# One-core block kernel: time-step work of the first stage ahead of the last S5 tile, more S5 buffers, residual reloads by GpSimd

## The chip, the cores and the metric
The kernel runs on one core of a Trainium2 chip. The metric is the time of one execution in device microseconds, the median of several runs. The engines that matter here are TensorE (PE in the rows; its weight loads are PEld), VectorE (DVE), ScalarE (ACT), GpSimd (POOL) and SyncE (SP), which only issues transfers. Each engine works through its own list of instructions in order.

## The reference
A sequence of 512 tokens with 16 meta tokens ahead of it (528 in all), 1024 wide, goes through a first block with two mixers side by side, then through a two-layer latent and context transformer. The change lies in the first block. Cut to what matters:
```python
xbc = silu(conv(...)); dt = softplus(dt_raw + dt_bias)       # SSD mixer
a_cs = cumsum(dt * -exp(a_log))                              # per chunk
y = y_diag + y_off + x * d;  y = rmsnorm(y * silu(z))
bu = u @ bb;  s = associative_scan(a, bu)                    # S5 mixer, complex, 64 groups
y5 = gelu(s_re @ c_re - s_im @ c_im + u * d_skip)
v = y5 @ w_glu + b_glu;  y5 = rmsnorm(v[:D] * sigmoid(v[D:]))
h = x + out_proj(concat(y, y5))                              # then an MLP
```

## The kernel before, in words
All matrix products are in float32, each as three matmuls of a high and a low part (`mm3`, lines 247 to 249). A weight tile arrives as `raw` (line 233, a transfer of SyncE, two buffers), ScalarE casts its high part `whi` (L239), VectorE subtracts for the low part `wlo` (L241).

The first stage follows `ORDER` (L207), a string that `build` works through letter by letter: x is one of twelve tiles of the convolution input with its silu (`xbc_proj`, L562 to L567), z one of four steps of the gate z (four silus, L592), P and S prepare and scan one of eight S5 tiles, d is the time-step projection with its softplus (`dt_proj`), e its cumulative sums (`dt_scan`, tiles acs and acsx), r the result of one S5 tile (`s5_result`). Engine order is made from this program order by a scheduler that weighs priorities and free buffers, and is then fixed.

`s5_scan` of a tile: angles (DVE f, ACT sine pieces L784 to L786), S on TensorE (L873) in two halves, each copied by ScalarE (L875) and permuted on TensorE (Sp, L877), rotated on VectorE (L878 to L880), the scan (L885), a permutation Zp (L888), rotation back (L889 to L891), y on TensorE (L894, L896), the copy ye (L899) and its write to a scratch tensor yD in DRAM (L900). `s5_result` reads it back in another layout as yt (L906), applies the gelu (L908), and makes high and low parts y50h, y50l and so on (L912, L913). These feed the gated linear unit, whose matmuls carry the names glug and glua and run over all eight y tiles. The tiles are numbered 0 to 7; tile 7 is the last.

The pools: `S2` is the number of 576-element buffers that S5 tiles, angles and yt share, `B4` that of the 1152-element ones. `hT` are the eight residual tiles. In the first stage they lend their space to S5 inputs and to z and the SSD state, and `ssd_out` loads the residual into them again (L698), for the addition behind the output projection (L958, L959).

ScalarE has a load instruction (ACT_TABLE_LOAD) ahead of a function whose table is not the one in use. Silu and sine follow each other here without one; exp and gelu each have their own.

Of the kernel before, what the change touches and what calls it, by code (L numbers as in the profile page):

```python
# [20 lines left out]
META = 16  # L21
# [169 lines left out]
class Builder:  # L191
# [12 lines left out]
    UB = (1, 0)  # L204
    MB = 0
    GL = (1, 2, 1, 2, 2)
    ORDER = "xPPxSPxSxPSxPxSPSzPSxxPSxzxxSrrzrxdrzrrrre"  # L207
    NF = (1, 0)
    SIDE = (1, 2, 2)
    FILL = (2, 2, 2, 2)  # L210
# [474 lines left out]
    def ssd_out(self):  # L685

        T = self.nc.tensor
        out = []
        for f in range(8):
            ps = self.mps(f"yT{f}")  # L690
            for i in range(1, 5):
                T.transpose(ps[:, (i - 1) * P:i * P],
                            self.ys[i, f // 4][:, (f % 4) * P:(f % 4 + 1) * P], self.C("ident"))
            out.append(self.split(f"mA{f}", ps, self.vec("g_ssd", f), tag="f"))
            self.tap(f"yssd{f}", out[-1][0].bitcast(F32))
        self.mixA = out
        for k in range(8):
            self.nc.sync.dma_start(self.hT[k][:, META:], self.I["xT"][k][:, META:])  # L698


    def s5_tables(self):
# [948 lines left out]
    def build(self, upto="all"):  # L1650
        tc = self.tc
        from contextlib import ExitStack
        with ExitStack() as st:
            self.kp = st.enter_context(tc.tile_pool(name="kp", bufs=1))
            self.wp = st.enter_context(tc.tile_pool(name="wp", bufs=3))
            self.dp = st.enter_context(tc.tile_pool(name="dp", bufs=1, space=DRAM))
            self.mod = {}
            self.tags = {"r": (TOK, 16), "f": (TOK, 16)}
            self.S2, self.B4 = 16, 8
            self.SM = 80  # L1660
            with tc.tile_pool(name="gp", bufs=4, space=PSUM) as self.gp, \
                    tc.tile_pool(name="sp", bufs=12) as self.sp, \
                    tc.tile_pool(name="mp", bufs=4, space=PSUM) as self.mp, \
                    tc.tile_pool(name="ap", bufs=1) as self.ap, \
                    tc.tile_pool(name="bp", bufs=1) as self.bp:
                self.setup()
                self.ys, self.xbcT, self.y5 = {}, {}, []
                self.in_proj()
                order = [8, 9, 10, 11, 0, 1, 2, 3, 4, 5, 6, 7]
                mats, z = {}, self.z_proj()  # L1670
                np_, ns = 0, 0
                for step in self.ORDER:
                    if step == "P":
                        mats[np_] = self.s5_prepare(np_)
                        np_ += 1
                    elif step == "S":
                        self.s5_scan(ns, mats.pop(ns))
                        ns += 1
                    elif step == "d":
                        self.dt_proj()  # L1680
                    elif step == "e":
                        self.dt_scan()
                    elif step == "x":
                        self.xbc_proj(order.pop(0))
                    elif step == "z":
                        next(z)
                    elif step == "r":
                        self.s5_result(len(self.y5))
                self.prev = [self.hT[2 * g + 1][:, :512] for g in range(2)]
                self.tags.update(b4=(1152, self.B4), s2=(576, self.S2))  # L1690
                side = self.ada(0, "s2", "b4", "s2", range(self.ADA1))
                g = self.glu()
                for i in range(5):
                    self.ssd_chunk(i)
                    for _ in range(self.GL[i]):
                        next(g)
                for _ in g:
                    pass
                self.out_proj(1, self.mixB, side)
                self.ssd_out()  # L1700
                self.out_proj(0, self.mixA, side)
                for _ in side:
                    pass
            for k in range(8):
                self.tap(f"hmix{k}", self.hT[k])
            self.SM = 16
            self.cxp = st.enter_context(tc.tile_pool(name="cxp", bufs=1))
            self.setup2()
            self.tags = {"h": (SEQ, 16), "gt": (SEQ, 14), "qk": (SEQ, 8), "vb": (SEQ, 4),
                         "kx": (SEQ + CTX, 2), "p": (SEQ, 4), "cv": (SEQ, 4), "yf": (SEQ, 4), "t": (SEQ, 6),  # L1710
                         "u": (SEQ + 30, 3), "b": (CTX, 3)}
            with tc.tile_pool(name="gp2", bufs=3, space=PSUM) as self.gp, \
                    tc.tile_pool(name="sp2", bufs=16) as self.sp, \
                    tc.tile_pool(name="mp2", bufs=5, space=PSUM) as self.mp, \
                    tc.tile_pool(name="ap2", bufs=1) as self.ap:
                side = self.ctx_stream()
                credit, step = 0.0, None
                for _ in self.mlp():
                    credit += 1.0
                    while credit > 0 and step != "last":  # L1720
                        step = next(side)
                        credit -= self.PACE.get(step, 0.0)
                for k in range(8):
                    self.tap(f"hmlp{k}", self.hT[k])
                self.second_block(side)


# [11 lines left out]
```

## Time and profile before
| | |
|---|---|
| runs | 2740.95, 2732.67, 2740.70 us; median 2740.7 |
| profiled execution | 2738.33 us, span 2736.6 us |
| busy in the span | TensorE 98%, VectorE 75%, ScalarE 43% |
| first stage | up to some 317 us of the span |

The times are those of whole executions; the span is what the trace covers of one of them. A busy share of 98% is a mean over the span: the gaps of TensorE have to be read from the stretch in which they lie.

### The profile page before, as it was taken

The numbers are of one execution on the slowest core, as the hardware profiler recorded it, in microseconds if no ns is written. First come the engines' busy times: TensorE is split into PE (matmuls) and PEld (weight loads), VectorE is DVE, ScalarE is ACT, GpSimd is POOL, SyncE is SP. The second block draws the span as 40 slices with busy tenths as digits, with TensorE's granted clock in tenths as the row PEclk, the third lists the DMA queues.
The fourth block names the chain that finished last, engine by engine and source line by source line (L and its number), as shares of the span: only waits on it lengthen the run. The fifth ranks groups of instructions, "written<-read, shape, count | busy, mean of one in ns | idle before, by whom it ended". The sixth has DMA issues, their size and how long they took to land.

```text
span 2736.6 us, 39800 instructions
## 1 busy us (share of the span) xinstructions
PE 2675.2 (98%) x15107; PEld 2269.9 (83%) x15107; DVE 2041.1 (75%) x3986; ACT 1165.5 (43%) x1961; POOL 6.0 (0%) x52
## 2 busy tenths in 40 slices
PE   8999899999999999999999999999999999999998
PEld 8898678788887898777788888888887777988887
DVE  7987678999885675898669888644769976655556
ACT  4443664433543553445454232322553454534333
POOL 0000000000000000000000000000000000000000
PEclk9999999999999999999999999999999999999999
DMA  6222435566332345322324446211342223232322
GB/s 210 72 82 76 120 124 169 165 205 196 124 108 96 121 148 181 97 89 85 106 85 148 149 153 217 93 61 63 106 145 92 89 66 96 92 97 87 109 93 77
DMA packets 157390, 321.02 MB, mean 117 GB/s; under 512 B 39760, under 2 KB 60688, under 8 KB 157200
## 3 DMA queue, kind: packets, MB, share of 16 engines
q1 hardware_dynamic: 157200, 318.49, 36.9%
q8 instruction: 119, 1.95, 0.3%
q14 instruction: 71, 0.58, 0.1%
HBM read 306.53 MB, written 9.54 MB: 115 GB/s over the span
## 4 chain that ended last, share of the span: by engine, by line
PE 78%; DVE 12%; DMA 4%; ACT 3%; issue 2%; SPq 0%; DVEq 0%; ACTq 0%; POOL 0%
PE lat1fu L247 3%; PE lat1fu L249 3%; PE lat1fu L248 3%; DVE wlo L241 3%; PE lat0fu L248 3%; PE lat0fu L247 3%; PE lat0fu L249 3%; PE dn L247 2%; PE dn L249 2%; PE dn L248 2%; PE up L248 2%; PE up L247 2%; PE up L249 2%; PE lat1d L248 1%; PE lat1d L247 1%
## 5 line engine op out<-in xcount | busy, mean ns | idle before, releaser
L239 ACT CAST whi<-raw 128x1024 fp32r<-128x1024 f32 (+3 forms) x486 | 456.7, 940 | 854.5 <-PE ctx0d L248 118.5
L241 DVE TENSOR_TENSOR wlo<-raw,whi 128x1024 fp32r<-128x1024 f32 (+3 forms) x486 | 526.7, 1084 | 196.2 <-ACT whi L239 190.3
L248 PE MATMUL ctx0fu<-ctx0fx,whi 128*128 128x256 f32 x352 | 99.7, 283 | 0.0
L249 PE MATMUL ctx0fu<-ctx0fx,wlo 128*128 128x256 f32 x352 | 99.6, 283 | 0.0
L247 PE MATMUL ctx0fu<-ctx0fx,whi 128*128 128x256 f32 x352 | 99.5, 283 | 0.0
L1137 DVE SCALAR_TENSOR_TENSOR lat0cv<-lat0u,vect,lat0cv 128x512 f32<-128x512 f32 x120 | 85.7, 746 | 0.5
L1137 DVE SCALAR_TENSOR_TENSOR lat1cv<-lat1u,vect,lat1cv 128x512 f32<-128x512 f32 x120 | 85.7, 744 | 0.5
L1468 DVE SCALAR_TENSOR_TENSOR lat0fc<-lat0fu,vect,lat0fc 128x511 f32<-128x511 f32 x44 | 32.9, 748 | 63.5 <-ACT lat0fc L1467 63.5
L248 PEld LDWEIGHTS ctx0fu<-ctx0fx,whi 128*128 128x128 f32 x352 | 67.4, 191 | 1.6
L247 PEld LDWEIGHTS ctx0fu<-ctx0fx,whi 128*128 128x128 f32 x352 | 67.4, 191 | 1.6
L249 PEld LDWEIGHTS ctx0fu<-ctx0fx,wlo 128*128 128x128 f32 x352 | 67.4, 191 | 0.0
L1467 ACT ACTIVATE lat0fc<-lat0fu,vect 128x512 f32<-128x512 f32 x44 | 34.3, 778 | 74.5 <-PE lat0fu L249 74.5
L1508 DVE SCALAR_TENSOR_TENSOR hT<-lat1d,mod1lat,hT 128x512 f32<-128x512 f32 (+1 forms) x40 | 25.5, 643 | 48.2 <-PE lat1d L249 48.0
L1137 DVE SCALAR_TENSOR_TENSOR cxcv<-cxu,vect,cxcv 128x256 f32<-128x256 f32 x120 | 52.6, 480 | 0.8
L249 PE MATMUL ctx0d<-ctx0fh,wlo 128*128 128x256 f32 x176 | 50.5, 288 | 0.5 <-DVE wlo L241 0.5
L248 PE MATMUL ctx0d<-ctx0fh,whi 128*128 128x256 f32 x176 | 50.4, 287 | 0.0
L247 PE MATMUL ctx0d<-ctx0fh,whi 128*128 128x256 f32 x176 | 50.0, 285 | 0.2 <-ACT whi L239 0.2
L988 DVE TENSOR_TENSOR hT<-hT,dn 128x512 f32<-128x512 f32 x40 | 27.4, 684 | 28.7 <-PE dn L249 28.7
L981 DVE SCALAR_TENSOR_TENSOR r<-up,rsbm 128x512 f32<-128x512 f32 x32 | 22.1, 690 | 31.7 <-PE up L249 31.7
L1508 DVE SCALAR_TENSOR_TENSOR hT<-lat0d,mod0lat,hT 128x512 f32<-128x512 f32 x32 | 23.9, 748 | 20.9 <-PE lat0d L249 20.9
L249 PE MATMUL cxg<-cxn1x,wlo 128*128 128x256 f32 x128 | 36.3, 284 | 0.4 <-DVE wlo L241 0.4
L247 PE MATMUL cxg<-cxn1x,whi 128*128 128x256 f32 x128 | 36.3, 284 | 0.0
(3104 smaller groups left out, 8944.2 us busy)
## 6 DMA issues: line engine op xcount, KB each, us to landing
raw<-in_p_in SPq DMA_DIRECT2D x100, 512.0 KB, 3.5
aw<-in_ada SPq DMA_DIRECT2D x192, 256.0 KB, 3.1
raw<-in_p_up SPq DMA_DIRECT2D x88, 512.0 KB, 3.5
raw<-in_p_dn SPq DMA_DIRECT2D x48, 384.0 KB, 3.0
raw<-in_w_up SPq DMA_DIRECT2D x32, 512.0 KB, 3.6
raw<-in_p_cn SPq DMA_DIRECT2D x48, 256.0 KB, 2.6
raw<-in_w_down SPq DMA_DIRECT2D x24, 384.0 KB, 3.0
raw<-in_p_out SPq DMA_DIRECT2D x18, 512.0 KB, 3.6
```

What stands on the lines that cost most here:

```text
L239: nc.scalar.copy(hi, raw)
L241: nc.vector.tensor_sub(lo, raw, hi.bitcast(F32))
L247: mm(ps, w[0], x[0], start=first, stop=False)
L248: mm(ps, w[0], x[1], start=False, stop=False)
L249: mm(ps, w[1], x[0], start=False, stop=last)
L981: V.scalar_tensor_tensor(r, ps, 0.0, rsb, op0=ALU.max, op1=ALU.mult)
L988: V.tensor_add(h[f], h[f], ps)
L1137: V.scalar_tensor_tensor(ac, u[:, k:k + n], self.vec(f"cdw{l}", 4 * k + i), ac, op0=ALU.mult, op1=ALU.add)
L1467: A.activation(u, ps[:, :n], AF.Identity, scale=wv(1), bias=self.vec(f"fdwb{l}", t))
L1468: V.scalar_tensor_tensor(u[:, 1:], ps[:, :n - 1], wv(0), u[:, 1:], op0=ALU.mult, op1=ALU.add)
L1508: V.scalar_tensor_tensor(x, ps, self.mod[l, kind][:, 40 + f:41 + f], x, op0=ALU.mult, op1=ALU.add)
```

## The change
`ORDER` moves d and e: d from ahead of the last three r, e from the very end, both to the place ahead of the last S. The eight reloads of hT are issued by GpSimd and no longer by SyncE. Two buffer counts grow, 16 to 17 and 8 to 10, and the scratch that is set aside for GpSimd's transfers is given a size of 4096.
```diff
--- before.py
+++ after.py
@@ -204,7 +204,7 @@
     UB = (1, 0)
     MB = 0
     GL = (1, 2, 1, 2, 2)
-    ORDER = "xPPxSPxSxPSxPxSPSzPSxxPSxzxxSrrzrxdrzrrrre"
+    ORDER = "xPPxSPxSxPSxPxSPSzPSxxPSxzxxdeSrrzrxrzrrrr"
     NF = (1, 0)
     SIDE = (1, 2, 2)
     FILL = (2, 2, 2, 2)
@@ -695,7 +695,7 @@
             self.tap(f"yssd{f}", out[-1][0].bitcast(F32))
         self.mixA = out
         for k in range(8):
-            self.nc.sync.dma_start(self.hT[k][:, META:], self.I["xT"][k][:, META:])
+            self.nc.gpsimd.dma_start(self.hT[k][:, META:], self.I["xT"][k][:, META:])
 
 
     def s5_tables(self):
@@ -1656,7 +1656,7 @@
             self.dp = st.enter_context(tc.tile_pool(name="dp", bufs=1, space=DRAM))
             self.mod = {}
             self.tags = {"r": (TOK, 16), "f": (TOK, 16)}
-            self.S2, self.B4 = 16, 8
+            self.S2, self.B4 = 17, 10
             self.SM = 80
             with tc.tile_pool(name="gp", bufs=4, space=PSUM) as self.gp, \
                     tc.tile_pool(name="sp", bufs=12) as self.sp, \
@@ -1726,7 +1726,8 @@
 
 
 def kernel(**inputs):
-    nc = bacc.Bacc("TRN2", target_bir_lowering=False, num_devices=1)
+    nc = bacc.Bacc("TRN2", target_bir_lowering=False, num_devices=1,
+                   dynamic_dma_scratch_size=4096)
     arrays = pack_inputs(inputs)
     ins = {k: nc.dram_tensor(f"in_{k}", v.shape, F32, kind="ExternalInput").ap()
            for k, v in arrays.items()}
```
What the engines' lists make of it is shown at three places. The lists of before and of the change are equal up to the scan of S5 tile 4 and again from the second glua tile on; between them the same work stands in another order. Names are those of the program with the number of the buffer behind them.

ScalarE, before, from the end of S5 tile 6 (its copy ye) over the sines and the two copies of S of tile 7:
```order
L899 COPY ye_2381<-y_2364 128x512
L784 ACTIVATE cs_2699<-f_2696 128x528
L785 ACTIVATE sn_2698<-f_2696 128x528
L786 ACTIVATE cs_2699<-cs_2699 128x528
L875 COPY S_2707<-S_0_2708 128x264
L875 COPY S_2707<-S_1_2718 128x264
L239 CAST whi_3258<-raw_3256 128x1024
L882 COPY f_2696<-mag_574 128x528
```
ScalarE in the change, ahead of the first copy of S of tile 7. In front of these rows stand the softplus and the copy of acs (L531); z are silus, acsx the exponentials of the cumulative sums:
```order
L592 ACTIVATE z_2889<-z_0_3087,rs1k 128x256
L533 ACT_TABLE_LOAD
L533 ACTIVATE acsx<-acs 128x160
L535 ACTIVATE acsx<-acsx 128x80
L542 COPY acTs<-acT 64x128
L239 CAST whi_3291<-raw_3289 128x1024
L592 ACT_TABLE_LOAD
L592 ACTIVATE z_2890<-z_0_3087,rs1k 128x256
L784 ACTIVATE cs_2813<-f_2810 128x528
L785 ACTIVATE sn_2812<-f_2810 128x528
L786 ACTIVATE cs_2813<-cs_2813 128x528
L875 COPY S_2821<-S_0_2822 128x264
```
The sines and the copy of S have moved behind the whole of d and e, and three table loads stand between the copy of acs and the copy of S; the second copy follows behind two more silus and a cast (rows L592, L592, L239).

ScalarE, before, in the gelu phase, from the readback of the second tile on (yt, L908 is the gelu):
```order
L908 ACTIVATE yt_2768<-yt_2768 128x512
L912 CAST y50h<-yt_2761 128x512
L499 ACTIVATE sp_3035<-dtv 128x80
L912 CAST y51h<-yt_2768 128x512
L908 ACTIVATE yt_2893<-yt_2893 128x512
L500 ACT_TABLE_LOAD
L500 ACTIVATE sp_3035<-sp_3035 128x80
L912 CAST y52h<-yt_2893 128x512
L908 ACT_TABLE_LOAD
L908 ACTIVATE yt_3057<-yt_3057 128x512
L908 ACTIVATE yt_3178<-yt_3178 128x512
L912 CAST y53h<-yt_3057 128x512
```
ScalarE in the change, from the copy ye of tile 7 on:
```order
L899 COPY ye_2872<-y_2855 128x512
L908 ACT_TABLE_LOAD
L908 ACTIVATE yt_2875<-yt_2875 128x512
L912 CAST y50h<-yt_2875 128x512
L908 ACTIVATE yt_2882<-yt_2882 128x512
L912 CAST y51h<-yt_2882 128x512
L908 ACTIVATE yt_3007<-yt_3007 128x512
L912 CAST y52h<-yt_3007 128x512
L908 ACTIVATE yt_3080<-yt_3080 128x512
L912 CAST y53h<-yt_3080 128x512
```
The pieces L499 and L500 of the softplus with their table loads no longer stand between the gelus; one load is left, ahead of the first gelu.

TensorE, before, from the first Sp of tile 7 (its S on either side, z behind it; the row list goes on with 23 more z matmuls before Zp):
```order
L877 MATMUL Sp_0_2714<-S_2707,cst 128x264
L873 MATMUL S_1_2718<-hT_88,P_2272 128x66 x4
L249 MATMUL z_0_3064<-whi_3122,xg5l 128x256
L247 MATMUL z_0_3064<-whi_3122,xg6h 128x256
L248 MATMUL z_0_3064<-wlo_3124,xg6h 128x256
L249 MATMUL z_0_3064<-whi_3122,xg6l 128x256
L877 MATMUL Sp_1_2724<-S_2707,cst 128x264
L247 MATMUL z_0_3064<-whi_3122,xg7h 128x256
L248 MATMUL z_0_3064<-wlo_3124,xg7h 128x256
L249 MATMUL z_0_3064<-whi_3122,xg7l 128x256
```
TensorE in the change, the same place:
```order
L249 MATMUL z_1_3088<-whi_3145,xg7l 128x256
L877 MATMUL Sp_0_2828<-S_2821,cst 128x264
L873 MATMUL S_1_2832<-hT_88,P_2272 128x66 x4
L877 MATMUL Sp_1_2838<-S_2821,cst 128x264
L888 MATMUL Zp_0_2846<-S_2821,cst 128x264
L888 MATMUL Zp_1_2850<-S_2821,cst 128x264
L894 MATMUL y_2855<-hT_88,M_1_637 128x64
L611 MATMUL bT_3230<-cst,xbcT_883 16x128
```
No z matmul is left from the first Sp to y; the last z stands ahead of it, and the transposes for the first SSD chunk (bT) follow on the first y matmul.

On SyncE the readback of tile 0 (yt, L906) now stands ahead of the write of tile 7's ye (L900), and the other seven behind it as before. On GpSimd the reload of tile 6's hT stands ahead of the memset that tile 7's scan needs (L883), and the other seven behind it.

## Rows read from the trace of the kernel before
Times are in microseconds from the start of the span.

**Rows 1.** Busy time of each engine by stretch.
```profile
core 0: us, PE busy (x) PEld busy (x) DVE busy (x) ACT busy (x) POOL busy (x), PEclk, DMA share, GB/s
266.00:269.00 3.00, 3.00 (x28) 3.00 (x27) 0.77 (x2) 2.36 (x5) 0.00 (x0) 1.00 0.54 143
290.00:295.00 5.00, 4.41 (x10) 3.27 (x11) 3.20 (x5) 4.95 (x8) 0.00 (x0) 0.50 1.31 221
310.00:850.00 540.00, 537.64 (x2712) 442.60 (x2711) 455.76 (x957) 241.18 (x414) 0.81 (x12) 1.00 0.46 151
```

**Rows 2.** TensorE's longest wait, 240 to 320 us: total, times, longest.
```profile
PE glug L247 <- ACT y50h L912: 7.6, 1, 7.6
```

**Rows 3.** The chain of waits from 282 us: start, length, what.
```profile
282.66 0.59 ACT ye L899
...
284.44 4.50 DMA yt<-yD
...
289.60 0.94 ACT y50h L912
```

**Rows 4.** TensorE in order of time, 245 to 318 us: start, length, line, tile.
```profile
245.79 0.28 PE L247 MATMUL dt<-xg0h,whi 128*16 128x264 f32 x1
...
265.47 0.39 PE L896 MATMUL y<-t,Y 128*128 128x64 f32 x2
...
271.55 0.71 PE L877 MATMUL Sp<-S,cst 128*128 128x264 f32 x2
...
282.24 0.39 PE L896 MATMUL y<-t,Y 128*128 128x64 f32 x2
...
305.55 0.39 PE L528 MATMUL acs<-dta,cst 16*128 16x16 f32 x2
...
317.09 0.39 PE L247 MATMUL glua<-y50h,whi 128*128 128x512 f32 x1
```

**Rows 5.** ScalarE in order of time, 266 to 308 us.
```profile
266.38 0.65 ACT L784 ACTIVATE cs<-f 128x528 f32<-128x528 f32 x1
...
267.99 0.37 ACT L875 COPY S<-S 128x264 f32<-128x264 f32 x1
...
274.10 1.04 ACT L239 CAST whi<-raw 128x1024 fp32r<-128x1024 f32 x1
275.05 0.83 ACT L592 ACTIVATE z<-z,rs1k 128x256 f32<-128x256 f32 x2
...
307.02 0.29 ACT L531 COPY acs<-acs 128x160 f32<-128x160 f32 x1 [1.46 <-PE acs L529]
307.35 0.34 ACT L533 ACTIVATE acsx<-acs 128x160 f32<-128x160 f32 x1
...
307.94 0.36 ACT L613 COPY bt<-bT 16x256 f32<-16x256 f32 x1
```

**Rows 6.** ScalarE in order of time, gelu phase.
```profile
292.42 1.28 ACT L500 ACT_TABLE_LOAD   x1
293.72 0.27 ACT L500 ACTIVATE sp<-sp 128x80 f32<-128x80 f32 x1
...
298.89 1.11 ACT L912 CAST y54h<-yt 128x512 fp32r<-128x512 f32 x1
...
300.44 1.08 ACT L912 CAST y55h<-yt 128x512 fp32r<-128x512 f32 x1
...
304.46 1.10 ACT L912 CAST y57h<-yt 128x512 fp32r<-128x512 f32 x1
```

**Rows 7.** VectorE in order of time, tile 7's scan.
```profile
273.40 1.22 DVE L241 TENSOR_TENSOR wlo<-raw,whi 128x1024 fp32r<-128x1024 f32 x1
274.53 1.25 DVE L885 TENSOR_TENSOR_SCAN S<-f,t 128x528 f32<-128x528 f32 x1
```

**Rows 8.** The reloads of hT by their line: issues, and time to landing.
```profile
L698 SPq DMA_DIRECT2D hT<-in_xT x8: 328/382/425, 267.9 to 469.3; - x8
...
DMA to landing us min/median/max: 2.6/3.3/4.8
```

**Rows 9.** VectorE in order of time, at 475 us.
```profile
474.91 0.69 DVE L958 TENSOR_TENSOR hT<-hT,ot 128x512 f32<-128x512 f32 x1
```

## The prediction

> **What bounds the kernel now.** I read three views in this order: busy time by stretch, the list of waits, and the chain of waits around the longest one. From 310 us on TensorE is busy 537.64 of 540.00 us [rows 1]: nothing in that stretch can take up a delay, so whatever the first stage loses or wins by 317 us stays in the total, and what the larger buffer counts can still win behind it is bounded by the 2.4 us that are missing there. The first stage does have slack. The longest wait of TensorE in it is 7.6 us in one piece: the first glug matmul waits for ScalarE's cast y50h [rows 2]. The chain says why: ye, the result of S5 tile 7, is copied at 282.66, written out, read back as yt by a transfer that ends at 288.94, put through the gelu and cast [rows 3]. No stage of that chain can start before tile 7 ends, so the end of tile 7 is the time to watch. The stall also costs clock: in 290 to 295 the granted clock is 0.50, the 1.2 GHz level, while TensorE is busy 4.41 of 5 us [rows 1]; ten matmuls at twice their length lose half of that, about 2.2 us.
>
> **The change part by part.** The letters d and e move ahead of the last S, so TensorE, ScalarE and VectorE get the time-step work (dt, softplus, cumulative sums) ahead of tile 7. The work is the same; its order decides. I follow it with durations of the rows from 245.79 on, where both kernels have done equal work (before starts on dt there, the change has dt behind it and 48 matmuls of xbc still to come).
>
> Step 1, to the end of acs. Before, tile 6 ends at 265.7 [rows 4]. The change has 14 z matmuls and the first half of tile 7's S less ahead of that point: 14 at 0.11 us (28 in 3.00 us, [rows 1]) and about 0.85, so minus 2.4. Against it I set 1.5 us of new idling, since the weight cast for the last xbc (1.04) comes behind silus of z at 0.42 each in ScalarE's order [rows 5]. Tile 6 then ends at 264.8. Behind it stand 66 z matmuls (7.3 us) and the transposes dtT (0.5); VectorE's softplus is hidden by these. acs starts at 272.6 and takes 1.47 (from 305.55 [rows 4] to its copy at 307.02 [rows 5]): 274.1.
>
> Step 2, the new wait. ScalarE's copy of S, which releases the first Sp of tile 7, stands behind this in its queue: acs copy 0.29, table load, silu 0.42, table load, exp 0.27, then a smaller exp and the copy acTs (0.2 each, my estimate for less than the shapes in the rows), weight cast 1.0, table load, silu 0.42, three sine pieces at 0.54, copy 0.3. With a table load at 1.28 [rows 6] and the others from [rows 5] that is 8.6 us, so the copy ends at 282.7. TensorE holds 24 z matmuls, acT and S against it, some 3.6 us, and then idles 5 us. Before, the same copy stood right behind the sines at 267.99 and TensorE had 33 z matmuls to do meanwhile.
>
> Step 3. The second copy of S comes behind two silus and a weight cast, 0.84 + 1.0 + 0.3: 284.85. From that Sp to the end of y before took from 271.55 to 282.5 [rows 4], 10.95 us, with a VectorE weight split of 1.13 us in it that held the scan [rows 7]. The change has one such split in the same chain, so I keep the length. But of its z matmuls, which filled TensorE before, none is left: the chain now runs with an idle TensorE, at the low clock for some of it. The rows without fillers alone would end 1.6 us earlier; y at half clock through would end 1.8 later. Tile 7 ends at 295.8 instead of 282.5: **+13.3**.
>
> Here the Trainium skill speaks, "ScalarE: Activation LUTs", section "What ACT_TABLE_LOAD costs": it gives about 1283 ns for the load and as much again for a drain, about 2.66 us a switch, and its rules advise doing all of one table set before switching, against which this change goes. This case's rows show the load at 1.28 and the next operation 0.02 us behind its end, 293.72 after 292.42 + 1.28 [rows 6], so they show no drain. By the page's figure the three switches in step 2 would cost 4.1 us more, and the time would be about 2751; by the row they cost what I put in.
>
> Step 4, the gelu phase. Before, from the end of ye (283.25, [rows 3]) to the end of cast y57h (305.56, [rows 6]) is 22.3 us. Inside it lie the time-step pieces of ScalarE with three table loads. The change has none there but the first; and yt of tile 0 is read back ahead of ye in the queue of SyncE, so its gelu and cast are done while the second transfer is under way. The other seven readbacks are still queued behind ye's write: the first of them lands 5.7 us after ye's end, as the first did before [rows 3]. From there seven pairs of gelu and cast at 1.55 (298.89 to 300.44, [rows 6]) are 10.85, and the copies that come between, one of bt at 0.36 [rows 5] and two of the SSD state (128x512, some 0.5 each by the gelus of that shape), are 1.4. Sum 17.95, so **-4.4**. The loads that sat here are not gone: they are the ones of step 2.
>
> Step 5, to the point where both orders meet again, glua's next tile, at 317.09 before [rows 4], 11.5 us after the cast. The change has 40 matmuls left there, transposes and a short wait for y57l. Its 40 matmuls at about 0.23 us are 9.2 (0.43 at half clock before, half of that here); with 2 us for the rest, an estimate, 11.3, so **-0.2**.
>
> The sum is 13.3 - 4.4 - 0.2 = +8.7 us.
>
> The other edits. The buffer counts 17 and 10 I cost at nothing: no wait of TensorE in the first stage is for a free buffer [rows 2], and the 2.4 us behind it are the most that they could win. The eight reloads of hT go from SyncE to GpSimd's queue, where nothing else stands for long: their start is at 267.9 to 469.3, they land after 2.6 to 4.8 us [rows 8], and the tile of the last four that is wanted first is wanted at 474.91 [rows 9], so the spare time is some 2 to 5 us. I cost them at nothing, since their issue takes 0.38 us of a queue with no later work that TensorE waits for. If GpSimd were late by more than the spare time, the residual additions would be late, and TensorE only once the PSUM buffers of the output projection are full. On SyncE the reload of tile 7's hT stood ahead of ye's write, waiting for tile 7 itself, so its going frees nothing but the first readback (counted above).
>
> The Trainium skill has a rule against that move too, "SBUF — State Buffer", section "SBUF: two separate sides": descriptors of a GpSimd transfer are written by GpSimd, which VectorE can lock out of their shared port. No run here shows a GpSimd transfer yet. VectorE is busy 455.76 of 540 us in that stretch [rows 1], so by the rule a reload could wait long; that is the last rival below.
>
> **Base.** The profiled execution took 2738.3 us, 1.7 more than its span of 2736.6, and 2.4 below the median of 2740.7. The forecast is 2738.3 + 8.7 = **2747 us**. A measurement of this kernel tells about 0.3%, 8.2 us, from no change: under 2732.5 is faster, over 2748.9 slower. So the forecast is a loss just too small to be told.
>
> **The rivals.**
> Slower, by the clock. If after the new 5 us of idling the granted clock stays at 0.50 through all of tile 7's y and into the glug phase, y ends 1.8 us later, and the ten matmuls at half clock are paid twice over, 2 us: 2751. For it: 0.50 behind the 7.6 us stall [rows 1, 2], and that TensorE here gets only short bursts, so that the clock may fall more than once. Against it: in the gelu phase TensorE has 1.4 us of work in each 1.55, and half of a wait for ScalarE costs nothing. It decides if y's matmuls stand at 0.50 throughout.
> Faster: tile 7 is not late. If ScalarE reached the S copies as early as TensorE could use them (TensorE, not ScalarE, sets acs and S), steps 1 to 3 give 0 to +2, and the -4.4 of step 4, the half clock (-2.2) and up to -2.4 from buffers are won: 2729 to 2736. For it: the dt work's gaps lie under z work, and the 7.6 us stall is the largest hole to fill. Against it: the rows of ScalarE's order above, 8.6 us in series. It decides if the idle time ahead of the first Sp is under 1 us.
> Slower, by the reloads. Reloads late by 5 to 10 us past their spare time would hold the output projection for 2 to 5 us beyond its buffers: 2749 to 2752. Against it: nothing but its own queue delays them.
>
> **How the numbers follow.** Forecast, 0.45: its own range is 2743 (no low clock, buffers win 2.4) to 2750 (y at half clock, late silus); 0.30 of it falls within 0.3% and 0.15 above. Clock rival 0.20: 0.16 above, 0.04 within. Faster rival 0.25: 0.15 below, 0.10 within. Reloads 0.10: 0.07 above, 0.03 within. Sums: faster 0.15, same 0.47, slower 0.38. The range 2733 to 2752 leaves out the better half of the faster rival and the upper end of the slower ones.
>
> **What the profile of the change would show.** Step 1: acs on TensorE at about 273, right behind z work. Step 2: an idle time of about 5 us ahead of the first Sp of tile 7, put down to ScalarE's S, with three table loads between acs copy and that copy. Step 3: idle times again ahead of the second Sp and of Zp, ye's copy ending near 296.5. Step 4: y57h cast 18 us after that, with no table load between the gelus, and a glug wait of some 3 us instead of 7.6. Step 5: glua's next tile near 326. The forecast is wrong if ye ends before 290, if ScalarE's chain is interrupted by waits that I left out (acs later than 276), or if TensorE idles on hT or the output projection past 460.

## The result and the profile after

The change takes 2752.33 us in the median of 4 runs (2751.26 to 2754.88), before takes 2738.9 in the median of 4 (2732.67 to 2740.95). The ratio of the runs is 1.0059, 95% interval [1.0044, 1.0074]; the medians lie 13.4 us apart. The kernel is slower by about half a per cent. The forecast was 2747, within 0.3% of before; the range ended at 2752, 0.3 us below what was measured.

The profiled execution took 2751.89 us with a span of 2750.0. Start times differ by up to some 3 us from execution to execution within the first 180 us, where both kernels have the same order, so I measure from the copy ye of S5 tile 3 (185.79 before, 185.00 after), the last tile in which both orders agree, to the glua tile at which they meet again. TensorE has the same work in that stretch. First before, then the change (columns: stretch, length, busy us and instructions of TensorE, its weight loads, VectorE, ScalarE, GpSimd, granted clock, DMA share, GB/s), and of the change four stretches in it:
```profile
185.79:317.09 131.30, 119.08 (x845) 104.45 (x845) 95.20 (x166) 64.75 (x107) 0.56 (x5) 0.96 0.37 102
```
```profile
185.00:332.11 147.11, 127.07 (x844) 108.36 (x844) 97.40 (x168) 70.14 (x113) 1.75 (x7) 0.91 0.34 92
285.00:290.00 5.00, 3.98 (x12) 2.95 (x12) 2.90 (x5) 2.56 (x6) 0.00 (x0) 0.50 0.29 88
290.00:295.00 5.00, 1.47 (x4) 1.17 (x4) 3.27 (x6) 0.63 (x1) 0.11 (x1) 0.50 0.48 143
295.00:300.00 5.00, 5.00 (x38) 4.35 (x37) 2.76 (x5) 0.00 (x0) 0.00 (x0) 0.81 0.00 0
305.00:310.00 5.00, 3.34 (x6) 1.61 (x6) 2.10 (x3) 3.71 (x5) 0.00 (x0) 0.50 1.33 229
```
131.30 has become 147.11, 15.8 us more. The same 844 or 845 matmuls are busy for 127.07 instead of 119.08 us, and idle time is 20.04 instead of 12.22. So about half of the loss, 8.0 us, is the same matmuls taking longer, and half, 7.8 us, is TensorE standing still. The clock column goes with it: 0.50 for ten microseconds from 285 and again in 305 to 310. An estimate of its part: in all its stretches at 0.50 TensorE is busy some 18.4 us in the change and 4.4 before; half of that is what the low level costs, 9.2 against 2.2 us, so 7.0 of the 8.0. Busy time over a stretch of equal work is the reading that the prediction's sum, made of waits and durations at full clock, lacked.

Not all of the 15.8 is the change's. Cut at the copy ye of tile 4, the stretch falls into two, before (first two rows) and in the change:
```profile
185.79:212.37 26.58, 24.65 (x193) 22.75 (x193) 21.41 (x36) 11.75 (x20) 0.11 (x1) 1.00 0.31 92
212.37:317.09 104.72, 94.43 (x654) 81.70 (x654) 73.79 (x131) 53.00 (x87) 0.45 (x4) 0.95 0.38 104
185.00:213.87 28.87, 26.16 (x192) 23.39 (x192) 20.50 (x36) 10.73 (x20) 0.11 (x1) 0.94 0.25 69
213.87:332.11 118.24, 100.92 (x654) 84.97 (x654) 76.90 (x133) 59.41 (x93) 1.64 (x6) 0.90 0.36 97
```
The first part is 2.3 us longer in the change, at a clock of 0.94 instead of 1.00. It varies with the execution: two runs below whose lists of TensorE and ScalarE are the change's in it take 32.17 us at a clock of 0.84 (the new ORDER alone) and 27.03 at 1.00 (the added matmuls). From tile 4's ye on, the change takes 13.5 us more than before, 6.5 of it busy and 7.0 idle; two traces of one kernel below agree there to 0.02 us. The experiments are therefore compared from tile 4's ye too.

The waits of TensorE in 240 to 345 us, where before had one wait of 7.6 [rows 2] (total, times, longest):
```profile
PE Sp L877 <- ACT S L875: 5.5, 3, 4.8
PE Zp L888 <- DVE S L885: 4.0, 2, 3.5
PE glug L247 <- ACT y50h L912: 3.7, 1, 3.7
PE xbc L247 <- ACT whi L239: 1.4, 1, 1.4
```
The glug wait is halved, as forecast. The 1.4 for xbc are the idling that step 1 had put at 1.5. Besides the rest of the glug wait there are now 4.8 us ahead of Sp (in a total of 5.5), and 3.5 ahead of Zp, where before had at most 0.5 in its filled chain.

ScalarE from the copy of acs on, which answers to [rows 5, 6]; start, length, line, tile, and in brackets the idle time before it:
```profile
276.87 0.29 ACT L531 COPY acs<-acs 128x160 f32<-128x160 f32 x1 [1.81 <-PE acs L529]
277.18 1.28 ACT L592 ACT_TABLE_LOAD   x1
278.48 0.47 ACT L592 ACTIVATE z<-z,rs1k 128x256 f32<-128x256 f32 x1
278.97 1.28 ACT L533 ACT_TABLE_LOAD   x1
...
281.87 1.28 ACT L592 ACT_TABLE_LOAD   x1
...
285.14 0.36 ACT L875 COPY S<-S 128x264 f32<-128x264 f32 x1
...
288.45 0.38 ACT L875 COPY S<-S 128x264 f32<-128x264 f32 x1 [1.27 <-PE S L873]
...
300.96 0.58 ACT L899 COPY ye<-y 128x512 f32<-128x512 f32 x1 [8.91 <-PE y L896]
...
306.23 0.63 ACT L908 ACTIVATE yt<-yt 128x512 f32<-128x512 f32 x1 [1.66 <-DMA yt<-yD]
...
316.57 0.58 ACT L678 COPY hT<-st 128x512 f32<-128x512 f32 x1 [1.76 <-PE st L675]
...
319.71 1.10 ACT L912 CAST y57h<-yt 128x512 fp32r<-128x512 f32 x1
```
Between the copy of acs at 276.87 and the end of the copy of S (285.14 + 0.36) lie 8.6 us, three of them table loads. The second copy of S ends 3.3 us behind the first, and waits for TensorE's S, not for ScalarE's own queue (idle 1.27). ye ends at 301.54; y57h at 320.81, 19.27 behind it.

TensorE at the places of [rows 4]:
```profile
275.40 0.39 PE L528 MATMUL acs<-dta,cst 16*128 16x16 f32 x2
...
285.56 1.25 PE L877 MATMUL Sp<-S,cst 128*128 128x264 f32 x2 [4.85 <-ACT S L875]
286.60 1.81 PE L873 MATMUL S<-hT,P 128*128 128x66 f32 x8
288.88 1.25 PE L877 MATMUL Sp<-S,cst 128*128 128x264 f32 x2 [0.47 <-ACT S L875]
293.66 2.10 PE L888 MATMUL Zp<-S,cst 128*128 128x264 f32 x4 [3.53 <-DVE S L885]
...
300.54 0.39 PE L896 MATMUL y<-t,Y 128*128 128x64 f32 x2
...
332.11 0.39 PE L247 MATMUL glua<-y50h,whi 128*128 128x512 f32 x1
```
The second half of S takes 1.81 us for 8 pieces, Sp 1.25, Zp 2.10: about twice what the same forms took with the fillers before (Sp 0.71, [rows 4]).

The reloads of hT from GpSimd's queue, answering to [rows 8]:
```profile
L698 POOL DMA_DIRECT2D hT<-in_xT x8: 536/536/670, 266.9 to 485.5; - x8
...
DMA to landing us min/median/max: 2.9/3.4/6.2
```
They are issued in 0.54 us each, land a little later (median 3.4), and no wait of TensorE in 380 to 560 us is for them.

### The profile page after: what moved, and what is told of

Same layout as the page of the kernel before. It is cut to its first block, busy times and chain, and to the rows that moved or that the text cites. A ratio compares the mean times of both kernels' runs of the same rounds, so it can differ in the third digit from the quotient of the medians.

```text
span 2750.0 us, 39807 instructions
## 1 busy us (share of the span) xinstructions
PE 2684.2 (98%) x15107; PEld 2275.7 (83%) x15107; DVE 2040.2 (74%) x3986; ACT 1170.2 (43%) x1965; POOL 10.3 (0%) x60
## 4 chain that ended last, share of the span: by engine, by line
PE 82%; DVE 10%; ACT 3%; DMA 3%; issue 2%; SPq 0%; DVEq 0%; ACTq 0%; POOL 0%
PE lat1fu L247 3%; PE lat1fu L248 3%; PE lat1fu L249 3%; PE lat0fu L247 3%; PE lat0fu L248 3%; PE lat0fu L249 3%; PE dn L247 2%; PE up L248 2%; PE dn L249 2%; PE dn L248 2%; PE up L249 2%; PE up L247 2%; DVE wlo L241 2%; PE lat1d L248 1%; PE lat1d L247 1%
## 5 line engine op out<-in xcount | busy, mean ns | idle before, releaser
L239 ACT CAST whi<-raw 128x1024 fp32r<-128x1024 f32 (+3 forms) x486 | 456.8, 940 | 853.5 <-PE ctx0d L248 119.3
L1468 DVE SCALAR_TENSOR_TENSOR lat0fc<-lat0fu,vect,lat0fc 128x511 f32<-128x511 f32 x44 | 32.9, 748 | 62.6 <-ACT lat0fc L1467 62.6
```

The costliest lines, as they stand in the source:

```text
L239: nc.scalar.copy(hi, raw)
L1468: V.scalar_tensor_tensor(u[:, 1:], ps[:, :n - 1], wv(0), u[:, 1:], op0=ALU.mult, op1=ALU.add)
```

## The experiments

**Which edit it is.** The kernel before with the new ORDER alone:
```diff
-    ORDER = "xPPxSPxSxPSxPxSPSzPSxxPSxzxxSrrzrxdrzrrrre"
+    ORDER = "xPPxSPxSxPSxPxSPSzPSxxPSxzxxdeSrrzrxrzrrrr"
```


> The kernel before with nothing but the new ORDER (d and e ahead of the last S); buffer counts and reload queue as before. Theory (ScalarE's order ahead of tile 7's S copy is the whole loss): 11 to 15 us over before, the next glua tile at 330 to 334, an idle time of 4 to 6 us ahead of the first Sp of tile 7. Rival (the larger pools or GpSimd's reloads carry a part of it): less than 6 us over before.

2757.2 us, ratio 1.0067 [1.0050, 1.0084]. Its stretch of equal work, to the same two marks:
```profile
185.26:217.43 32.17, 28.70 (x192) 25.74 (x192) 20.51 (x36) 10.75 (x21) 0.11 (x1) 0.84 0.23 62
217.43:337.29 119.86, 99.24 (x655) 84.21 (x655) 76.88 (x133) 60.76 (x98) 0.44 (x4) 0.90 0.35 96
```
152.03 us in all, 20.7 over before: 8.9 busy, 11.9 idle. Of the 4.9 us more than in the change, 3.3 lie ahead of tile 4's ye, at the lower clock; from there on it is 119.86, 15.1 over before and 1.6 over the change. ORDER alone loses all of it and some more; the idle time ahead of the first Sp is 4.9. The rival falls. The total, 18.1 over before, is beyond the theory's range too: the three other edits give back a small part of what ORDER costs. The next one is their turn, the change with the old ORDER:
```diff
-    ORDER = "xPPxSPxSxPSxPxSPSzPSxxPSxzxxdeSrrzrxrzrrrr"
+    ORDER = "xPPxSPxSxPSxPxSPSzPSxxPSxzxxSrrzrxdrzrrrre"
```


> The changed kernel with the old ORDER: buffer counts, scratch size and reload queue stay changed. Theory: within 3 us of before, since no wait is for a buffer and the reloads are hidden; at most 1.3 us for each table load that its list has more between the gelus. Rival (buffers or reloads): 5 to 12 us over before.

2735.11 us, ratio 0.9990 [0.9980, 1.0000]:
```profile
209.77:312.81 103.04, 95.67 (x653) 82.10 (x653) 74.30 (x132) 55.45 (x89) 1.65 (x6) 0.95 0.39 101
```
103.04 us from tile 4's ye on, 1.7 below before (130.24 from tile 3's, 1.1 below). The wait for y50h is 3.3 instead of 7.6, since the reload of tile 7's hT no longer stands ahead of the first readback (issued at 274.69, ahead of tile 7's ye; before at 283.64, behind it); ScalarE has one table load more in the gelu phase. The theory stands, the rival (buffers, reloads) falls. Run once more with more rounds:

> The second experiment's kernel once more, beside the one above on the same chip, to tell 0.1% from nothing. If the larger buffers and the moved reloads help by themselves: 1 to 4 us below before, the interval clear of 1. If not: within 1 us of before.

2736.73 us, ratio 0.9992 [0.9983, 1.0001], and from tile 4's ye on:
```profile
209.89:312.95 103.06, 95.58 (x653) 81.95 (x653) 74.27 (x132) 55.44 (x89) 1.64 (x6) 0.95 0.39 101
```
Neither branch is met cleanly: 2.4 us below before, but the interval just reaches 1. The total can't tell 0.1%; the stretch, 1.7 us below before in both traces and 1.6 between the change and ORDER alone, speaks for a gain of that size with either ORDER. All of it lies behind tile 7's ye.

**What the order costs: table loads.** In the change, the four exponentials of dt_proj and dt_scan become copies; four lines of this kind:
```diff
-        A.activation(ex[:, :160], acs, AF.Exp)
+        A.activation(ex[:, :160], acs, AF.Copy)
```


> The changed kernel with the four exponentials of dt_proj and dt_scan replaced by scaled copies, so that no table is loaded for them; the outputs of the time step are other numbers, the amount of work is the same. Theory (the table switches in series ahead of tile 7's S copy are the larger part of the new wait): that copy 5 us earlier than in the change (at about 280), 6 to 9 us below the change in all. Rival (the place in the queue and the missing filler work, not the loads): copy 1 to 2 us earlier, at most 3 us below the change.

2747.32 us, ratio 1.0033 [1.0020, 1.0046], 5.0 below the change:
```profile
210.56:324.77 114.21, 101.00 (x655) 85.09 (x655) 76.80 (x133) 51.63 (x87) 1.65 (x6) 0.91 0.38 101
```
114.21 us from tile 4's ye on, 4.0 below the change and 9.5 over before (141.79 from tile 3's, 5.3 below the change). The copy of S comes 67.0 us behind tile 4's ye (277.60 - 210.56) instead of 71.3: 4.2 earlier, near the theory's 5. The gain in all falls between the two ranges. The loads are a third of the loss, not the larger part; 9.5 us stay without a single one of them ahead of tile 7.

**What the order costs: the place of the copies.** In the change, e moves behind the last S:
```diff
-    ORDER = "xPPxSPxSxPSxPxSPSzPSxxPSxzxxdeSrrzrxrzrrrr"
+    ORDER = "xPPxSPxSxPSxPxSPSzPSxxPSxzxxdSerrzrxrzrrrr"
```


> The changed kernel with d ahead of the last S and e directly behind it (d S e). In ScalarE's list the first copy of S of tile 7 then stands right behind the sines again. Theory: no idle time over 1 us ahead of the first Sp, tile 7 ends at 283 to 288, the gelu phase keeps its missing loads, the time is 2731 to 2740, at or a little below before. Rival (the dt work ahead of tile 7 costs the filler matmuls whatever ScalarE's order is): tile 7 ends past 292 and the time is over 2744.

2742.82 us, ratio 1.0011 [1.0001, 1.0022]. The stretch from tile 4's ye on, and ScalarE at tile 7:
```profile
214.10:319.94 105.84, 95.86 (x654) 81.86 (x654) 76.01 (x133) 57.83 (x92) 1.64 (x6) 0.97 0.40 109
```
```profile
272.33 0.65 ACT L784 ACTIVATE cs<-f 128x528 f32<-128x528 f32 x1
273.95 0.35 ACT L875 COPY S<-S 128x264 f32<-128x264 f32 x1
...
289.93 0.58 ACT L899 COPY ye<-y 128x512 f32<-128x512 f32 x1 [1.80 <-PE y L896]
```
The copy of S stands behind the sines again, no Sp waits over 0.3 us, and 12.4 of the 13.5 us are gone (105.84), although six of the change's seven table loads up to the first gelu are still there, in other places. So the place of the time-step work costs most, not its loads as such. The same edit also brings back fillers: 35 z matmuls stand between the first Sp and Zp, where the change has none, so the run doesn't take the place of the copies and the fillers apart. The forecast of the theory was too good by some microseconds, and neither range is met: ye starts at 289.93, 75.8 behind tile 4's ye and 5.5 later than before, since two loads and the softplus still stand ahead of the sines.

**What the order costs: the clock.** In the change, matmuls of no use on what is there already, ahead of the first Sp and of Zp:
```diff
+            if m == 7 and q == 0:
+                dm = self.mps("dm0")
+                for _ in range(24):
+                    T.matmul(dm[:, :160], self.C("perm"), self.acs160, start=True, stop=True)
...
+        if m == 7:
+            dm = self.mps("dm1")
+            for _ in range(9):
+                T.matmul(dm[:, :HALF], self.C("perm"), S[:, hf[1]], start=True, stop=True)
```


> The changed kernel with matmuls whose result nobody uses, put where TensorE idles in tile 7's chain: 24 of 160 columns on the copied acs ahead of the first Sp, 9 of 264 columns on S ahead of Zp. They read only what is there already and are meant to keep the granted clock up. Theory (the low clock behind the new idle time makes the second half of S, Sp, Zp and the start of the glug phase longer): the granted clock stays at 1.00 from 275 to 300, the second copy of S comes 1.3 us behind the first instead of 3.3, Zp takes 1.1 instead of 2.1, ye ends 2 to 4 us earlier after tile 3's ye than in the change, the time is 2 to 4 us below the change. Rival (ScalarE and VectorE alone set that chain): under 1 us.

2752.88 us, ratio 1.0045 [1.0028, 1.0062]. Stretches, then TensorE (dm are the added ones), then the scan on VectorE:
```profile
185.10:212.13 27.03, 24.64 (x192) 22.68 (x192) 20.49 (x36) 10.86 (x20) 0.11 (x1) 1.00 0.26 73
212.13:328.98 116.85, 107.65 (x721) 92.31 (x720) 76.75 (x133) 59.62 (x94) 1.64 (x6) 0.96 0.37 98
275.00:295.00 20.00, 19.28 (x131) 17.64 (x131) 10.18 (x19) 11.33 (x19) 0.11 (x1) 1.00 0.24 68
```
```profile
276.64 6.74 PE L879 MATMUL dm<-acs,cst 128*128 128x160 f32 x48
284.16 0.61 PE L882 MATMUL Sp<-S,cst 128*128 128x264 f32 x2
284.60 1.00 PE L874 MATMUL S<-hT,P 128*128 128x66 f32 x8
286.07 0.71 PE L882 MATMUL Sp<-S,cst 128*128 128x264 f32 x2
292.21 1.16 PE L897 MATMUL Zp<-S,cst 128*128 128x264 f32 x4 [0.71 <-DVE S L894]
```
```profile
290.90 1.26 DVE L894 TENSOR_TENSOR_SCAN S<-f,t 128x528 f32<-128x528 f32 x1 [2.90 <-PE dm L889]
```
The granted clock stays at 1.00, the second half of S takes 1.00 instead of 1.81, Sp 0.61 and 0.71 instead of 1.25, Zp 1.16 instead of 2.10. The two Sp stand 1.9 us apart instead of 3.3. From the second Sp to ye, though, it is 12.2 us against 12.1 in the change: the scan writes S, which the nine added matmuls read, and so waited for them some 2.0 us past the memset that it otherwise follows (that ended at 288.88). The next glua tile comes 143.88 behind tile 3's ye, 3.2 us earlier than in the change, though TensorE has more to do. But 1.8 of the 3.2 lie ahead of tile 4's ye, far from the first added matmul; from there on it is 116.85, 1.4 less than in the change. So the theory is right on the clock and on the pieces. By its own mark, tile 3's ye, ye comes 2.8 us earlier, within its 2 to 4; but behind tile 4's it is only 1.0, with the added matmuls themselves in the way. The scheduler also put 18 z matmuls among and around the added ones, which in the change stand ahead of the first Sp. In the total nothing of it is seen, and the rival's number holds: the median is that of the change, and this trace has 2.2 us of waiting in an SSD chunk later (yd for VectorE's dd) that the change hasn't.

**Can the time-step work stand elsewhere?** Three other places in the change's ORDER. Ahead of tile 6's pieces:
```diff
+    ORDER = "xPPxSPxSxPSxPxSPSzPSdexxPSxzxxSrrzrxrzrrrr"
```


> The changed kernel with d and e two tiles earlier, ahead of the pieces of tile 6 (... S z P S d e x x P S x z x x S ...). The exponentials and their table loads then lie in the stretch of tiles 5 and 6, and ScalarE's list has none between tile 6's ye and tile 7's. Theory (what costs is the time-step work in ScalarE's queue ahead of the last S5 tile, where nothing is left to cover it): tile 7 ends as far behind tile 3 as before or up to 3 us later, the gelu phase keeps its 3 to 4 us, the time is 0 to 7 us below before. Rival (the loads cost the same wherever they stand in the S5 stage): 4 us or more over before.

2763.89 us, ratio 1.0088 [1.0073, 1.0103]. From tile 1's ye, since the order differs earlier (before: 185.10 from there to the glua tile), and two stretches:
```profile
130.78:340.60 209.82, 183.96 (x1265) 160.95 (x1264) 143.40 (x248) 93.07 (x152) 2.19 (x12) 0.91 0.32 85
265.00:285.00 20.00, 19.20 (x150) 17.59 (x149) 16.38 (x29) 9.00 (x18) 0.11 (x1) 1.00 0.19 43
285.00:300.00 15.00, 7.29 (x41) 6.00 (x40) 6.49 (x11) 4.54 (x9) 0.78 (x2) 0.63 0.51 157
```
209.82, 24.7 over before, half of it busy time (183.96 against 171.85). The theory falls, and the rival takes it by number, but its reason doesn't reach tile 7: ScalarE's last load stands at 258.12, and tile 6's sines start at 271.84. TensorE is busy 19.20 of 20 us until 285, and 7.29 of 15 behind it, at a clock of 0.63. Its z and xbc matmuls, which wait for nothing but weights, have been done early (the last starts at 283.89), and tile 7 runs with nothing beside it.

Ahead of tile 3's pieces:
```diff
+    ORDER = "xPPxSPxSdexPSxPxSPSzPSxxPSxzxxSrrzrxrzrrrr"
```


> The changed kernel with d and e ahead of tile 3's pieces (... S x P S x S d e x P S ...), with two table loads less than in the change. Theory: as with d and e ahead of tile 6, 0 to 8 us below before; if the idle time that the loads make there is smaller, 1 to 2 us below that version. Rival (the loads cost the same wherever they stand): 4 us or more over before.

2772.66 us, ratio 1.0119 [1.0103, 1.0135]. The earlier, the worse, with two loads less than in the change: the theory falls again, and here too the rival's number holds.

At the very end:
```diff
+    ORDER = "xPPxSPxSxPSxPxSPSzPSxxPSxzxxSrrzrxzrrrrrde"
```


> The changed kernel with d and e at the very end of ORDER (... x z x x S r r z r x z r r r r r d e). The dt matmuls are then TensorE's filler in tile 7's chain, and all eight gelus but the last stand ahead of the softplus in ScalarE's list. Theory (what counts is how much work that waits for nothing is left to TensorE while tile 7 and the gelus run, and that ScalarE's copies of S stand right behind the sines): tile 7 ends within 1 us of before, measured from tile 3's ye, y50h comes 4 us earlier behind it, the time is 2 to 6 us below before. Rival (the softplus chain, now behind the gelus, holds the first SSD chunk): an idle time of over 3 us ahead of acs or yd, and no gain.

2740.32 us, ratio 1.0003 [0.9994, 1.0012]: the same as before. TensorE's waits:
```profile
PE glug L247 <- ACT y50h L912: 4.4, 1, 4.4
PE yd L652 <- DVE dd L648: 2.2, 1, 2.2
```
ye starts 98.4 us behind tile 3's ye, 1.5 later than before instead of within 1 (0.9 of it lies ahead of tile 4's ye), y50h ends 4.0 behind ye's end (7.3 before). What it wins there it loses on yd, 2.2 us, nearer the rival: the softplus now ends behind the gelus.

**Gelus ahead of tile 7.** Seven, then two of the r ahead of the last S, d and e at the end:
```diff
+    ORDER = "xPPxSPxSxPSxPxSPSzPSxxPSxzxxrrrrrrrSzxzrde"
```


> The changed kernel with seven of the eight r ahead of the last S and d, e at the end (... x z x x r r r r r r r S z x z r d e). Gelu and readback of tiles 0 to 6 then stand ahead of tile 7 in ScalarE's list, and glug matmuls fill TensorE in tile 7's chain. Theory (filler work): tile 7 ends 6 to 10 us later behind tile 6's ye than before, but only one gelu is left behind it, and the next glua tile comes 2 to 8 us earlier than before, measured from tile 3's ye. Rival (ScalarE's queue ahead of the S copy decides, as in the change): tile 7 ends over 12 us later and the time is over before.

2747.10 us, ratio 1.0025 [1.0014, 1.0035]. The wait of Sp:
```profile
PE Sp L877 <- ACT S L875: 14.2, 3, 13.7
```
Thirteen microseconds in one piece: the copy of S stands behind seven gelus and casts and four loads. ye starts 39.3 us behind tile 6's ye (16.8 before), the rival. Two gelus:
```diff
+    ORDER = "xPPxSPxSxPSxPxSPSzPSxxPSxzxxrrSrzrxzrrrrde"
```


> The changed kernel with two of the eight r ahead of the last S and d, e at the end (... x z x x r r S r z r x z r r r r d e). Two gelus, with a table load each way, stand ahead of tile 7's sines; z and dt matmuls cover them, and ten glug and glua matmuls stand in tile 7's chain. Theory: ScalarE's copy of S comes some 5 us later behind tile 6's ye than before, covered by 85 z and dt matmuls (some 10 us); tile 7 ends 2 to 5 us later, the gelu phase is 3 to 6 us shorter, the time is 0 to 5 us below before. Rival (each thing put ahead of tile 7 on ScalarE costs its own length at the end): 3 to 6 us over before.

2758.35 us, ratio 1.0063 [1.0050, 1.0076]: the rival again, and more. Sp waits 2.8 us, ye starts 32.2 behind tile 6's ye, and its stretch of equal work is 145.92 us at a mean clock of 0.89. Two gelus ahead of the copy cost more than their own length here. Yet seven cost less than two: with seven, the stretch from tile 7's ye to the glua tile takes 21.4 us instead of 34.4 before, with two 32.9.

**A load in the gelu phase.** The second experiment's kernel with the exponential of a_log on VectorE:
```diff
-        av = self.small("av", 16)
-        A.activation(av, self.row("a_log"), AF.Exp)
+        av = self.exp_acc("av", self.row("a_log"), 16)
```


> The second experiment's kernel (old ORDER, the other three edits) with the exponential of a_log computed by the kernel's own polynomial on VectorE, so that its table load (L520) and the load back to gelu behind it are gone from the gelu sequence. Theory (between ye of tile 7 and the cast y57h ScalarE sets the pace, so a load there costs its whole length): y57h ends 2.5 us earlier behind ye than in that kernel, and the time is 2 to 3 us below it, some 4 to 6 us below before. Rival (y57h is not what the next matmuls wait for): no change against that kernel.

2735.80 us, ratio 0.9989 [0.9980, 0.9998]. y57h, here and in the run beside it (ye ends at 284.25 here, at 280.74 there):
```profile
302.09 1.07 ACT L911 CAST y57h<-yt 128x512 fp32r<-128x512 f32 x1
```
```profile
301.45 1.12 ACT L912 CAST y57h<-yt 128x512 fp32r<-128x512 f32 x1
```
y57h ends 18.9 us behind ye's end instead of 21.8, 2.9 less, as expected. But the next glua tile comes 130.91 behind tile 3's ye, against 129.66 there: nothing is won. Against the kernel beside it the rival holds. It is the only run whose interval lies wholly below before, by 0.1%.

## Why the prediction was wrong

**What held.** That the end of tile 7 decides, that ScalarE's order ahead of it is the new wait, that the gelu phase gets shorter but by less, that the loss reaches the end: all in the trace. So the path was right, and sizes on it were not. Step 2 was exact: 8.6 us forecast from acs copy to the copy of S, 8.6 measured, with 4.85 us of idling forecast as 5. Table loads take 1.28 us each here too, and an operation starts 0.02 us behind one (278.48 after 277.18 + 1.28), so that the drain which the Trainium skill, "ScalarE: Activation LUTs", section "What ACT_TABLE_LOAD costs", adds to each is not seen in this trace. The advice of that page's section "Rules for kernel authors" to do all of one set before switching does bear: the loads are 4.0 of 13.5 us. Step 5 came out by its number, 11.3. The reloads are hidden, so the rival built on them falls. So does the one in which tile 7 is not late: TensorE idles 4.85 us ahead of the first Sp. Buffers and reloads at nothing: 1.7 us of gain in the stage, most of it the earlier first readback, which step 4 had counted; in the total 2 to 4 us, by intervals that just reach 1.

**What failed: the sizes of three terms, step 3 first.** The sum was +8.7, for the stretch from where both kernels have done equal work (245.79 before, 246.53 in the change) to the glua tile. Measured, it is 71.30 before and 85.58 in the change: +14.3. By the steps:
- Step 3: "I keep the length". It set 1.6 us less for the missing fillers against 1.8 more for the low clock, and so put the two together at nothing. The second copy of S came 3.3 us behind the first instead of 2.15, and from there to the end of y it took 12.1 instead of 10.95. **+2.3.** The clock explains it: 0.50 in 285 to 295, with S, Sp and Zp, which gate each other, at twice their lengths; with the added matmuls they took their old ones. An estimate from that run: 1.4 us between the two Sp and 1.9 behind them (the 2.0 that the scan waited for the added matmuls, less the 0.1 that the way to ye was longer), so some 3 us for the clock in tile 7's chain.
- Step 1: acs starts 28.9 us behind the start of the stretch (275.40 - 246.53), forecast 26.8. **+2.1.** Of it 1.3 lie ahead of the end of tile 6's y (266.80), and 0.8 in the 66 z matmuls and transposes: z matmuls start 0.12 us apart, not 0.11, since the 28 that were counted in 3.00 us are records of 0.28 that overlap.
- Step 4: from ye's end to the end of y57h it took 19.3 us, forecast 17.95 (-3.0 instead of -4.4). **+1.3.** The second readback came 1.0 us earlier than put in; but the pace of gelu and cast was 1.63 us instead of 1.55, and ScalarE waited 1.76 for the state's matmul, which TensorE, at 0.50 in 305 to 310, reached late.

8.7 + 2.1 + 2.3 + 1.3 = 14.4, which is the 14.3 within the rounding of the steps. The way from there to the total is in part luck: 1.5 us more lie ahead of the stretch, by the clock between tile 3 and tile 4; the first 185 us were 0.8 shorter in this trace than before, and the later stretch 1.6 shorter (2419.5 us before, 2417.9 here, 2417.1 to 2427.3 in the traces of this case). That leaves 13.4, the difference of the spans.

**Two more points that were wrong, without weight in the sum.** The weight split that "held the scan" in step 3 [rows 7] held it hardly: the memset that the scan needs as well ended at 274.37, and the scan started at 274.53. In the change, with no split at that place, the scan starts 0.9 us behind VectorE's last rotation (291.34 to 292.25), before 1.05. And the rival by the clock, whose 2751 came nearer than the forecast, had the mechanism in the wrong place: it was to be decided by y at 0.50 throughout, but all of y except its first matmuls stood at full clock, 3.5 us long. That its number came near is luck.

**What stays open.** What a full clock in tile 7's chain would win in the total: the run that kept it gained 1.4 us in the stage and nothing at the end. How the position of the copies and the fillers share the 12.4 us: the one run that gives back both doesn't tell. Why the clock falls between tile 3 and tile 4 in some executions and not in others that do the same list. That the new ORDER alone costs 4.9 us more than the change needs no other order to explain it: 3.3 are that clock, and 1.6 lie behind tile 7's ye, where the first readback is late again (TensorE waits 8.1 us for y50h, 3.7 in the change).

## What to carry to other kernels

A serial chain over three engines needs two things of the engine that bounds the kernel: that nothing long stands ahead of the chain's small copies on the other engines, and that work which waits for nothing is left to fill the chain's gaps. Moving other work ahead of the chain takes away both, and the earlier the time-step work was moved here, the dearer it got (13, 24 and 33 us over before in the total). Measure it over a stretch of equal work and split it into idle and busy: the rise in busy time of the same matmuls is the part that a list of waits doesn't show, and here it was half. And start that stretch behind everything that varies between executions of one list: from tile 3 it showed 3.2 us for the added matmuls, from tile 4 it shows 1.4.

## What the runs showed of the hardware that was not expected

Short bursts did not bring the clock back in the change: TensorE was busy 3.98 of 5 us in 285 to 290 and 1.47 of 5 in 290 to 295, and the granted clock was 0.50, the 1.2 GHz level, throughout; it was 0.81 as a mean over the 5.00 busy us of 295 to 300. With the added matmuls in the gaps it stayed at 1.00 over the same pieces. The same list of TensorE and ScalarE, from tile 3's ye to tile 4's, ran at a mean clock of 1.00, 0.94 and 0.84 in three traces, and took 27.03, 28.87 and 32.17 us. GpSimd's issue of a reload takes 0.54 us against SyncE's 0.38, and its transfer lands 0.1 us later in the median (3.4 against 3.3), 1.4 in the worst case (6.2 against 4.8).
